# A two-layer hybrid trunk on one core: residual loads spread, gate-stage work moved to VectorE, attention's weights requested one output earlier, the last product in two halves

## The chip, the cores and the metric

One NeuronCore of a Trainium2 chip runs the whole program in one launch. Five engines run side by side, each through its own instruction stream in order: TensorE (PE, with its weight loads shown apart as PEld), VectorE (DVE), ScalarE (ACT), GpSimd (POOL) and SyncE (SP), which here only issues DMA transfers. The metric is the device time of one execution in microseconds, less being better.

## The reference

The activations are `x` (1024 tokens, 1024 features). Layer 0 mixes with an RWKV-7 group and a gated DeltaNet group, layer 1 with chunked softmax attention. Each layer then has a squared-ReLU MLP and a gated addition of a per-layer embedding:

```python
h = rmsnorm(x, norm_mix_g[i])
...                                   # mixer: even layers two recurrent groups, odd layers attention
x = x + mix
hf = rmsnorm(x, norm_ffn_g[i])
x = x + jnp.square(jax.nn.relu(hf @ mlp_w1[i])) @ mlp_w2[i]
x = x + rmsnorm(p[i] @ ple_w_proj[i], ple_norm_g[i]) * jax.nn.sigmoid(x @ ple_w_gate[i])
```

All is float32. The kernel splits each operand into a high part (type fp32r) and a low rest and forms a product from three matmuls.

## The kernel before

The residual lives transposed: eight *rows* of 128 features by 1024 tokens, `x[0]` to `x[7]`, each worked on in two halves of 512 tokens (`hs[0]`, `hs[1]`). `x[0..2]` share the tile `xw0`, `x[3..5]` the tile `xw1`, and `x[6]`, `x[7]` are tiles of their own; the order and the profile print them without the digit, as `xw` and `x`.

A layer is a mixer and then `tail(i, ...)`, which the change is in. The tail does, in this order:

- the mixer's output projection, which leaves the residual in DRAM as `xh` (first halves) and `xm` (second halves);
- the MLP's first product with seven block products in place of eight (`product`), its results stored as `hb` by ScalarE's DMA queue (`store`, L1427) after the row factor `rs` (`normed`, L1422);
- the load of the residual back from DRAM into `x` (L1542 and L1543, SyncE);
- the MLP's second product: a first group done plainly (`plain`, sixteen half outputs of 12 matmuls, each added to `x` by VectorE in `add_to`, L1550, after which `between` starts loads and splits for what follows), and then sixteen blocks in the seven-product form;
- the gate stage: eight outputs `n` of 24 matmuls a half. `ev_gate` takes a half from PSUM: tanh (ScalarE, L1644), the embedding `pn` loaded (L1646) and multiplied by the row factor `prs` (GpSimd, L1647), combined (VectorE, L1648), added to `x` (L1649), stored. In layer 0 it also scales and splits the new row for attention (`xg`, L355 on ScalarE and L356 on VectorE) and adds its squares into `accs` (L1659 on ScalarE, L1660 on GpSimd).

Layer 1's attention starts with the products of `xg` with `wq` (`attn_in`); the first head pair's `wq` is loaded from within layer 0's gate stage (`load_qkv`: load L1878, high part L1879 on ScalarE, low part L1880 on VectorE) into the tiles `xw0` (high) and `xw1` (low), those of rows 0 to 5. After three token groups `row_stats` forms the sums of `accs` on TensorE (`st`) and VectorE turns them into factors (`ms`, L378 and following); only then can the three PSUM banks be emptied.

A list scheduler with its own timeline orders each engine's instructions, so a change in one place can shift orders in another. Every product of the program is recorded at one line (L180), every transpose at L195. Pools give out buffers in turn; an instruction waits until the last user of its buffer is done. DMA transfers report through a small set of semaphores that SyncE's and ScalarE's queues share in turn.

Of the kernel before, what the change touches and what calls it, by code (L numbers as in the profile page):

```python
# [11 lines left out]
AF = mybir.ActivationFunctionType  # L12
ALU = mybir.AluOpType
# [7 lines left out]
NK = D // P  # L21
HB = 512
# [90 lines left out]
class Trunk:  # L113
# [213 lines left out]
    def dense_part(self, w, acts, evac, order=None):  # L327
        hi, lo = w
        order = order or list(range(len(acts)))
        ps = self.bank()  # L330
        for k in order:
            x = acts[k]
            self.mm3(ps, hi[:, k * P:(k + 1) * P], lo[:, k * P:(k + 1) * P], x[:, 0, :], x[:, 1, :],
                     k == order[0], k == order[-1])
            yield 0
        if self.late is not None:
            self.late.append(lambda: evac(ps))
            n = len(self.late)
            if n in self.plan:
                self.plan[n]()  # L340
            if n == max(self.plan):
                late, self.late = self.late, None
                for f in late:
                    f()
        else:
            evac(ps)
# [866 lines left out]
    def tail(self, i, xsrc):  # L1213
# [9 lines left out]
        nc, tc, a = self.nc, self.tc, self.a  # L1223
        V, A, G = nc.vector, nc.scalar, nc.gpsimd
        last = i == 1
        hs = [slice(0, HB), slice(HB, T)]
        with ExitStack() as es:
            self.psd = 2 * self.psd[0:1] + 6 * [es.enter_context(self.pool(f"psdt{i}", 6, space=PSUM))]
            pB = es.enter_context(self.pool(f"actB{i}"))
            pB = [pB.tile([P, 2, T], F32R, tag=f"r{q}", name="r") for q in range(8)]  # L1230
# [5 lines left out]
            def place(dt, far=False, tag="a"):  # L1236
                if far:
                    return late.tile([P, 2, T], dt, tag=tag, name="late")
                return self.act([P, 2, T], dt, tag)
# [4 lines left out]
            def ring(views):  # L1244
                state = [0]

                def f():
                    state[0] += 1
                    return views[(state[0] - 1) % len(views)]
                return f  # L1250
# [5 lines left out]
            def tiles_x(dt):  # L1256
                xw = [self.xp.tile([P, 3, T], dt, tag=f"xw{q}", name=f"xw{q}") for q in range(2)]
                return ([xw[k // 3][:, k % 3, :] for k in range(6)] +
                        [self.xp.tile([P, T], dt, tag=f"x{k}", name=f"x{k}") for k in (6, 7)])
# [11 lines left out]
            accs = [self.accp.tile([P, HB], F32, tag=f"acc{hf}", name="acc") for hf in range(2)]  # L1271
# [13 lines left out]
            def weights(src, raw, hl):  # L1285
                nc.sync.dma_start(out=raw, in_=src)
                split(hl, raw)
                return hl[:, 0], hl[:, 1]
# [80 lines left out]
            for n in range(NK):  # L1369
# [3 lines left out]
                else:  # L1373
                    w = self.w_next if (i, n) == (0, 2) else weights(a[f"w_out{i}"][n], wr[n % 2], wo[n % 2])
# [7 lines left out]
            scr = ring([v for t in lt[0:2] for v in quarters(t)])  # L1382
            rs = self.pre.tile([P, T], F32, tag="ph", name="rs")
            sq = {}
# [3 lines left out]
            def product(p, m, banks):  # L1388
                c, first = prep[p][1][m], chain[m] not in banks
                if first:  # L1390
                    banks[chain[m]] = self.bank()
                ps = banks[chain[m]]
                for j in range(4):
                    o, z = slice(j * P, j * P + P), cmb[m][j]
                    self.mm3(ps, c[:, 0, o], c[:, 1, o], z[:, 0], z[:, 1], first and j == 0, j == 3, not first)
                return ps
# [94 lines left out]
            for p in range(16):  # L1491
# [5 lines left out]
                for q, m in enumerate(order):  # L1497
                    ps = product(p, m, banks)
# [28 lines left out]
                    if (p, q) in sums:  # L1527
                        n = sums.index((p, q))
# [9 lines left out]
                        V.tensor_tensor(rs, rs, rs, op=ALU.mult)  # L1538
                    yield 0
            x = tiles_x(F32)  # L1540
            for k in range(NK):
                nc.sync.dma_start(out=x[k][:, hs[0]], in_=self.xh[k])  # L1542
                nc.sync.dma_start(out=x[k][:, hs[1]], in_=self.xh2[k])  # L1543
            xf = pB
            areas[6], areas[2], areas[7], areas[3], areas[4] = pq[8:12], pq[12:16], cmb[4], pq[0:4], pq[4:8]
            braw = ring([self.accp.tile([P, HB], F32, tag=f"acc{q}", name="braw") for q in range(2)] + quarters(place(F32)))
            areas[1], areas[5] = [[c for q in qs for c in parts(place(F32R, True, f"r{q}"))] for qs in ((2, 3), (0, 1))]
# [24 lines left out]
            todo2 = [lambda: raws2(0)] + [lambda m=m: prepare2(0, m) for m in order]  # L1572

            def start_blocks(n, hf):
                for _ in range(2 if n < 4 else 1):
                    if todo:
                        todo.pop(0)()
                if n >= 4 and todo2:
                    todo2.pop(0)()
            yield from plain(0, h0, start_blocks)  # L1580
            for f in todo + todo2:
                f()
# [5 lines left out]
            xf = [pB[q] for q in (4, 6, 0, 2, 5, 7, 1, 3)]  # L1588
# [4 lines left out]
            for n in range(NB + 4):  # L1593
# [3 lines left out]
                for s, m in enumerate(order):  # L1597
# [3 lines left out]
                    ps, c = banks[chain[m]], prep2[n][1][m]  # L1601
                    for j, slot in enumerate(slots):
                        o, z = slice(j * P, j * P + P), areas[m][slot]
                        self.mm3(ps, c[:, 0, o], c[:, 1, o], z[:, 0], z[:, 1], first and j == 0, slot == slots[-1], not first)
                    e, hf = goes[m]
# [24 lines left out]
            prs = self.pre.tile([P, T], F32, tag="ph", name="prs")  # L1630
            pn2 = self.pre.tile([P, 2, HB], F32, tag="pl", name="pn")
# [6 lines left out]
            scr = ring(quarters(lt[3]))  # L1638

            def ev_gate(n):  # L1640
                def f(hf, ps):
                    sl = hs[hf]
                    sg = scr()
                    A.activation(sg, ps, AF.Tanh, scale=0.5)  # L1644
                    pn = pn2[:, hf]
                    nc.sync.dma_start(out=pn, in_=self.pnd[n][:, hf, :])  # L1646
                    G.tensor_tensor(pn, pn, prs[:, sl], op=ALU.mult)  # L1647
                    V.scalar_tensor_tensor(sg, sg, 1.0, pn, op0=ALU.add, op1=ALU.mult)  # L1648
                    V.tensor_tensor(x[n][:, sl], x[n][:, sl], sg, op=ALU.add)  # L1649
                    if last:  # L1650
                        nc.sync.dma_start(out=a["out"][n, :, sl], in_=x[n][:, sl])
                    else:
                        nc.sync.dma_start(out=self.xd[n][:, sl], in_=x[n][:, sl])
                        if hf == 0:
                            xg.append(place(F32R, tag="b" if n < 2 else "a"))
                        self.split_scaled(xg[n], x[n][:, sl], self.vec("mixg", 8 + n), sl)
                        if n:
                            sq = scr()
                            A.activation(sq, x[n][:, sl], AF.Square)  # L1659
                            G.tensor_tensor(accs[hf], accs[hf], sq, op=ALU.add)  # L1660
                        else:
                            A.activation(accs[hf], x[n][:, sl], AF.Square)
                return f
            wl = ring(halves(lt[1]))

            def load_gate(n):

                far = n > 1 and not last
                raw = wl() if far else raw_b()
                return weights(a["w_gate"][i, n], raw, lt[2 * (n % 2)] if far else place(F32R))  # L1670
            w = {n: load_gate(n) for n in range(2)}
            for n in range(NK):
                if n == NK - 1 and not last:
                    self.wq = self.load_qkv(0, wl)
                yield from self.dense(w.pop(n), xf, ev_gate(n))
                if n + 2 < NK:
                    w[n + 2] = load_gate(n + 2)
            if not last:
# [507 lines left out]
```

## Time and profile before

| | |
|---|---|
| time, median of 3 runs | 3074.66 us (3072.01 to 3075.01) |
| the profiled execution | 3086.63 us |
| its span | 3084.8 us |
| TensorE busy | 2970.1 us, 96% |
| VectorE busy | 2209.9 us, 72% |
| ScalarE busy | 1486.2 us, 48% |
| GpSimd busy | 552.9 us, 18% |
| mean granted TensorE clock | 0.974 |

Times are microseconds from the span's start. In a row of the timeline the first two numbers are start and duration; the brackets give how long the engine had been idle and what released it. A row of the windows lists the busy time of each engine with its instruction count, then the granted TensorE clock, the busy share of the DMA engines and what they moved. In this execution layer 0's tail ends at about 1694, layer 1's attention runs from there to about 2310, and layer 1's tail to the end.

### The profile page before, as it was taken

The numbers are of one execution on the slowest core, as the hardware profiler recorded it, in microseconds if no ns is written. First come the engines' busy times: TensorE is split into PE (matmuls) and PEld (weight loads), VectorE is DVE, ScalarE is ACT, GpSimd is POOL, SyncE is SP. The second block draws the span as 40 slices with busy tenths as digits, with TensorE's granted clock in tenths as the row PEclk, the third lists the DMA queues.
The fourth block names the chain that finished last, engine by engine and source line by source line (L and its number), as shares of the span: only waits on it lengthen the run. The fifth ranks groups of instructions, "written<-read, shape, count | busy, mean of one in ns | idle before, by whom it ended". The sixth has DMA issues, their size and how long they took to land.

```text
span 3084.8 us, 47290 instructions
## 1 busy us (share of the span) xinstructions
PE 2970.1 (96%) x17254; PEld 2457.1 (80%) x17254; DVE 2209.9 (72%) x4546; ACT 1486.2 (48%) x2957; POOL 552.9 (18%) x985
## 2 busy tenths in 40 slices
PE   8999999999999999999999999999999999999999
PEld 6777777777777888788887988898878888888887
DVE  7556766667758777788887676676768777788883
ACT  4333433434437555544444465565757555544441
POOL 5434442443500000000005111111210000000002
PEclk9899999999999999999999999999999999999999
DMA  4212112212346444754424211110256444654433
GB/s 145 64 55 62 54 49 75 61 55 68 110 157 227 162 150 151 262 166 151 151 95 131 70 44 40 43 61 23 75 181 223 163 154 153 237 190 150 150 103 116
DMA packets 194857, 368.49 MB, mean 119 GB/s; under 512 B 46800, under 2 KB 49088, under 8 KB 194624
## 3 DMA queue, kind: packets, MB, share of 16 engines
q1 hardware_dynamic: 163808, 309.35, 31.4%
q10 hardware_dynamic: 30816, 56.11, 4.7%
q8 instruction: 136, 2.23, 0.3%
q14 instruction: 97, 0.79, 0.1%
HBM read 268.86 MB, written 96.53 MB: 118 GB/s over the span
## 4 chain that ended last, share of the span: by engine, by line
PE 71%; DVE 14%; DMA 6%; ACT 4%; issue 2%; POOL 1%; SPq 0%; ACTq 0%; DVEq 0%; POOLq 0%
PE dps L180 57%; PE ch L180 2%; PE po L180 2%; DVE act L1283 2%; PE pm L180 1%; PE iz L180 1%; PE pt L195 1%; DMA late<-in_w 1%; PE sn L180 1%; PE tp L180 1%; DMA late<-hd 1%; DVE late L1431 1%; DMA wraw<-in_w_out 1%; PE py L180 1%; DVE wlo L307 1%
## 5 line engine op out<-in xcount | busy, mean ns | idle before, releaser
L180 PE MATMUL dps<-r,act 128*128 128x512 f32 x3720 | 872.9, 392 | 2.0 <-DVE xw L1550 0.8
L180 PEld LDWEIGHTS dps<-r,act 128*128 128x128 f32 x3720 | 698.0, 188 | 157.0 <-issue 1.2
L180 PE MATMUL dps<-xg,whi 128*128 128x512 f32 x1280 | 436.0, 421 | 11.2 <-ACT whi L306 7.4
L1647 POOL TENSOR_TENSOR pn<-pn,prs 128x512 f32<-128x512 f32 x32 | 47.3, 1483 | 1542.6 <-ACT prs L389 1419.5
L180 PE MATMUL dps<-wq,act 128*128 128x384 f32 x1536 | 307.8, 347 | 13.8 <-DVE vs L1909 6.0
L180 PEld LDWEIGHTS dps<-xg,whi 128*128 128x128 f32 x1280 | 236.2, 197 | 62.2 <-ACT whi L306 7.6
L180 PEld LDWEIGHTS dps<-wq,act 128*128 128x128 f32 x1536 | 269.6, 193 | 17.7 <-DVE vs L1909 7.6
L180 PE MATMUL dps<-xg,wlo 128*128 128x512 f32 x640 | 260.7, 407 | 2.6 <-DVE wlo L307 2.6
L1282 ACT CAST act<-act 128x512 fp32r<-128x512 f32 (+2 forms) x281 | 159.3, 600 | 142.0 <-PE dps L180 59.8
L1283 DVE TENSOR_TENSOR act<-act 128x512 fp32r<-128x512 f32 (+2 forms) x281 | 180.1, 669 | 4.6 <-ACT act L1282 4.6
L180 PE MATMUL dps<-act 128*128 128x512 f32 x720 | 176.5, 393 | 2.0 <-DVE late L1404 2.0
L1282 ACT CAST act<-late 128x512 fp32r<-128x512 f32 x210 | 123.7, 620 | 100.4 <-PE dps L180 73.8
L180 PE MATMUL dps<-late,act 128*128 128x512 f32 x672 | 166.6, 392 | 0.0
L180 PEld LDWEIGHTS dps<-act 128*128 128x128 f32 x720 | 136.2, 189 | 32.1 <-DVE late L1404 2.4
L1283 DVE TENSOR_TENSOR act<-late,act 128x512 fp32r<-128x512 f32 x210 | 139.1, 687 | 31.1 <-ACT act L1282 30.9
L180 PEld LDWEIGHTS dps<-xg,wlo 128*128 128x128 f32 x640 | 125.0, 195 | 32.5 <-DVE wlo L307 3.8
L180 PEld LDWEIGHTS dps<-late,act 128*128 128x128 f32 x672 | 126.0, 188 | 27.7
L180 PE MATMUL dps<-xw,act 128*128 128x512 f32 x576 | 145.9, 392 | 0.2 <-ACT act L1282 0.2
L1550 DVE TENSOR_TENSOR xw<-xw,dps 128x512 f32<-128x512 f32 x192 | 130.0, 682 | 17.3 <-PE dps L180 17.2
L306 ACT CAST whi<-wraw 128x1024 fp32r<-128x1024 f32 (+1 forms) x79 | 81.8, 1035 | 107.6 <-PE dps L180 77.1
L180 PEld LDWEIGHTS dps<-xw,act 128*128 128x128 f32 x576 | 107.9, 188 | 24.4 <-ACT act L1282 0.7
L180 PE MATMUL po<-ptile,vs 128*128 128x256 f32 (+1 forms) x576 | 106.8, 295 | 15.5 <-ACT ptile L352 9.7
(488 smaller groups left out, 5600.7 us busy)
## 6 DMA issues: line engine op xcount, KB each, us to landing
hb<-late ACTq DMA_DIRECT2D x196, 256.0 KB
act<-hb SPq DMA_DIRECT2D x158, 256.0 KB
late<-in_w SPq DMA_DIRECT2D x60, 512.0 KB
act<-in_w SPq DMA_DIRECT2D x112, 256.0 KB
wraw<-in_w_in SPq DMA_DIRECT2D x55, 512.0 KB
braw<-hb SPq DMA_DIRECT2D x80, 256.0 KB
wraw<-in_w_out SPq DMA_DIRECT2D x21, 512.0 KB
wraw<-in_w_qkv SPq DMA_DIRECT2D x21, 512.0 KB
```

Of the source, the lines that this page charges most:

```text
L180: return self.begin(self.nc.tensor.matmul(out, lhsT, rhs, start=start, stop=stop, skip_group_check=again))
L195: return self.begin(self.nc.tensor.transpose(out, in_, ident))
L306: nc.scalar.copy(hi, raw)
L307: nc.vector.tensor_tensor(lo, raw, hi.bitcast(F32), op=ALU.subtract)
L1282: A.copy(hi, s)
L1283: V.tensor_tensor(lo, s, hi.bitcast(F32), op=ALU.subtract)
L1431: V.tensor_tensor(t, u, v, op=ALU.subtract)
L1550: V.tensor_tensor(x[n][:, hs[hf]], x[n][:, hs[hf]], ps, op=ALU.add)
L1647: G.tensor_tensor(pn, pn, prs[:, sl], op=ALU.mult)
```

## The change

Four edits, all in `tail` but one line of `dense_part`. The residual's rows 0 to 2 are loaded where all eight were; the others are each requested after the first half of an output of the plain group, three outputs ahead, and pinned behind what was traced before them on SyncE. In the gate stage the two GpSimd operations go to VectorE. `load_qkv(0, ...)` is called before output 6 instead of before output 7. In layer 1 the second half of the last gate product is computed as two products of 256 tokens, each evacuated on its own (`ev_end`).

```diff
     def dense_part(self, w, acts, evac, order=None):
-        ps = self.bank()
+        ps = self.bank()[:, 0:acts[0].shape[-1]]
...
-            for k in range(NK):
-                nc.sync.dma_start(out=x[k][:, hs[0]], in_=self.xh[k])
-                nc.sync.dma_start(out=x[k][:, hs[1]], in_=self.xh2[k])
-            xf = pB
+
+            def load_res(n):
+                for hf, src in enumerate((self.xh[n], self.xh2[n])):
+                    tc.keep_in_program_order(nc.sync.dma_start(out=x[n][:, hs[hf]], in_=src))
+            for n in range(3):
+                load_res(n)
...
             def start_blocks(n, hf):
+                if hf == 0 and n + 3 < NK:
+                    load_res(n + 3)
...
-                    G.tensor_tensor(pn, pn, prs[:, sl], op=ALU.mult)
+                    V.tensor_tensor(pn, pn, prs[:, sl], op=ALU.mult)
...
-                            G.tensor_tensor(accs[hf], accs[hf], sq, op=ALU.add)
+                            V.tensor_tensor(accs[hf], accs[hf], sq, op=ALU.add)
...
+            def ev_end(c, ps):
+                sg, n = scr()[:, 0:HB // 2], NK - 1
+                A.activation(sg, ps, AF.Tanh, scale=0.5)
+                if c.start == HB:
+                    pn = pn2[:, 1]
+                    nc.sync.dma_start(out=pn, in_=self.pnd[n][:, 1, :])
+                    V.tensor_tensor(pn, pn, prs[:, hs[1]], op=ALU.mult)
+                V.scalar_tensor_tensor(sg, sg, 1.0, pn2[:, 1, c.start - HB:c.stop - HB], op0=ALU.add, op1=ALU.mult)
+                V.tensor_tensor(x[n][:, c], x[n][:, c], sg, op=ALU.add)
+                nc.sync.dma_start(out=a["out"][n, :, c], in_=x[n][:, c])
...
-                if n == NK - 1 and not last:
+                if n == NK - 2 and not last:
                     self.wq = self.load_qkv(0, wl)
-                yield from self.dense(w.pop(n), xf, ev_gate(n))
+                if last and n == NK - 1:
+                    yield from self.dense_part(w[n], [z[:, :, hs[0]] for z in xf], lambda ps: ev_gate(n)(0, ps))
+                    for q in (2, 3):
+                        c = slice(q * HB // 2, (q + 1) * HB // 2)
+                        yield from self.dense_part(w[n], [z[:, :, c] for z in xf], lambda ps: ev_end(c, ps))
+                else:
+                    yield from self.dense(w.pop(n), xf, ev_gate(n))
```

By the changed kernel's line numbers the residual's loads are L1544, `add_to` L1552, the product with `prs` L1651, the two operations behind it L1652 and L1653, the sum of squares L1664, and the low parts of attention's weights L1901. TensorE's order in the middle of attention comes out of the scheduler differently too.

## The prediction

> **What bounds the kernel now.** I read the totals first, then who TensorE waited for in the four places that the diff touches, then short windows around each wait.
>
> ```profile
> span 3084.8 us, 47290 instructions
> PE 2970.1 (96%) x17254; PEld 2457.1 (80%) x17254; DVE 2209.9 (72%) x4546; ACT 1486.2 (48%) x2957; POOL 552.9 (18%) x985
> ```
>
> TensorE is busy for 96% of the span, so only time in which it stands still or runs slowly can be saved, and the tail stages have little of that. TensorE's waits there, one answer each for 1240 to 1340, 1560 to 1720 (two rows) and 2640 to 2760 (columns: total us, times, longest):
>
> ```profile
> PE dps L180 <- DVE late L1404: 2.0, 1, 2.0
> ...
> PE dps L180 <- ACT act L355: 4.5, 1, 4.5
> PE dps L180 <- DVE vs L1909: 2.8, 1, 2.8
> ...
> PE dps L180 <- DVE r L1283: 0.7, 1, 0.7
> ```
>
> The first and last lie where the residual is loaded (layer 0, layer 1); the other two lie where layer 0's gate stage hands over to attention. Windows around them show what follows such a wait (width; busy us of PE, PEld, DVE, ACT, POOL; granted TensorE clock; DMA share; GB/s):
>
> ```profile
> 1283.00:1287.00 4.00, 2.76 (x13) 1.92 (x11) 0.74 (x3) 0.63 (x1) 0.00 (x0) 1.00 1.05 389
> 1287.00:1292.00 5.00, 4.28 (x12) 3.38 (x13) 4.17 (x8) 1.26 (x2) 0.00 (x0) 0.66 0.74 281
> ...
> 1694.00:1698.00 4.00, 3.85 (x12) 3.34 (x13) 2.85 (x4) 1.78 (x4) 2.24 (x3) 0.57 0.73 223
> ...
> 1714.00:1718.00 4.00, 4.00 (x16) 4.00 (x16) 2.73 (x12) 0.00 (x0) 1.04 (x1) 0.58 0.02 4
> 1720.00:2310.00 590.00, 543.99 (x3387) 510.15 (x3386) 422.38 (x1325) 361.93 (x897) 92.82 (x84) 0.97 0.20 64
> ...
> 2676.00:2680.00 4.00, 3.74 (x16) 3.10 (x17) 2.54 (x4) 0.42 (x1) 0.00 (x0) 1.00 1.05 396
> ```
>
> After the waits of 2.0, 4.5 and 2.8 us the clock falls to 0.66, 0.57 and 0.58 in the window behind; after the 0.7 us it does not. TensorE is busy in those windows, so the lost clock is lost time: (1 - 0.66) x 5 = 1.7, (1 - 0.57) x 4 = 1.7, (1 - 0.58) x 4 = 1.7 us. A wait that goes takes its slow stretch along.
>
> The Trainium skill's page "TensorE: Matmul & The Clock Gate" (section "Why this matters for your kernels") warns of idle gaps above about 3 us only. By it the slow stretches behind 2.0 and 2.8 us would not hang on those gaps, and the result would be 3.4 us later than mine. The trace disagrees: clock 0.66 behind a gap of 2.0.
>
> **Residual's loads.** Layer 0's stall, step by step:
>
> ```profile
> 1280.13 0.54 SPq L1543 DMA_DIRECT2D x<-xm  x1
> ...
> 1285.34 0.33 ACTq L1427 DMA_DIRECT2D hb<-late  x1
> 1285.71 0.63 ACT L1410 ACTIVATE late<-late 128x512 f32<-128x512 f32 x1 [3.29 <-DMA x<-xm]
> ```
>
> ScalarE could not issue a store until the last residual half had landed, 5 us after its issue; L1410 stood behind that store, VectorE's L1404 behind L1410, and TensorE behind L1404. At 389 GB/s the transfers were saturated. On SyncE's queue, at the start of the first plain group of layer 0, `xw1`/`x6`/`x7` being residual rows 3 to 7, before stands
>
> ```order
> L1542 DMA xw_12789<-xh 128x512
> L1543 DMA xw_12789<-xm 128x512
> L1542 DMA x_12790<-xh 128x512
> L1543 DMA x_12790<-xm 128x512
> L1542 DMA x_12791<-xh 128x512
> L1543 DMA x_12791<-xm 128x512
> L1482 DMA act<-hb 128x512 x2
> ```
>
> and now, from the same place (rows 0 to 4 go out ahead of it in both):
>
> ```order
> L1482 DMA act<-hb 128x512 x2
> L1482 DMA braw<-hb 128x512
> L1441 DMA w_12896<-in_w 128x512 x2
> L1544 DMA xw_12789<-xh 128x512
> L1544 DMA xw_12789<-xm 128x512
> L1482 DMA act<-hb 128x512 x2
> L1441 DMA w_12986<-in_w 128x512 x2
> L1544 DMA x_12791<-xh 128x512
> L1482 DMA act<-hb 128x512
> L1544 DMA x_12791<-xm 128x512
> L1482 DMA act<-hb 128x512
> ```
>
> Six loads of 256 KB leave the burst: 1.57 MB at 389 GB/s is 4.0 us, more than ScalarE's 3.3 us wait. I take layer 0's stall as gone: 2.0 + 1.7 = **3.7 us** (bounds 0 and 3.7). Layer 1 has the same burst (396 GB/s) and 0.7 us: **0.7 us** (bounds 0 and 0.7). Late next could be row 6: it comes last of all, behind twelve further transfers and the braw pair before which it now stands:
>
> ```profile
> 1306.76 0.32 SPq L1482 DMA_DIRECT2D braw<-hb  x1
> ...
> 1319.87 0.69 DVE L1550 TENSOR_TENSOR x<-x,dps 128x512 f32<-128x512 f32 x1
> ```
>
> Issued at about 1306.8 and used at 1319.9, it has 13 us, against 5 for a landing in the burst. Free.
>
> **Gate stage.** VectorE, ScalarE and GpSimd in 1620 to 1680, grouped by line (count | busy us, mean ns | idle before, releaser):
>
> ```profile
> L1648 DVE SCALAR_TENSOR_TENSOR late<-late,pn 128x512 f32<-128x512 f32 x11 | 14.7, 1334 | 5.6 <-ACT late L1644 5.6
> L1649 DVE TENSOR_TENSOR xw<-xw,late 128x512 f32<-128x512 f32 x10 | 11.9, 1188 | 0.3
> L356 DVE SCALAR_TENSOR_TENSOR act<-xw,vecs,act 128x512 fp32r<-128x512 f32 x11 | 9.5, 860 | 6.7 <-ACT act L355 6.5
> ...
> L1880 DVE TENSOR_TENSOR wq<-late,wq 128x1024 fp32r<-128x1024 f32 x2 | 2.7, 1382 | 2.3 <-DMA xd<-xw 2.3
> ...
> L1660 POOL TENSOR_TENSOR acc<-acc,late 128x512 f32<-128x512 f32 x10 | 17.8, 1780 | 7.9 <-ACT late L1659 7.9
> L1647 POOL TENSOR_TENSOR pn<-pn,prs 128x512 f32<-128x512 f32 x12 | 17.7, 1479 | 43.0 <-DMA pn<-pnd 39.4 <-DMA xd<-xw 3.6
> ```
>
> The end of the kernel shows the pace of a half output (ScalarE's tanh comes every 5.49 us) and the same VectorE work with GpSimd idle, 0.69 us instead of 1.19:
>
> ```profile
> 3074.03 0.60 ACT L1644 ACTIVATE late<-dps 128x512 f32<-128x512 f32 x1 [4.89 <-PE dps L180]
> ...
> 3079.52 0.60 ACT L1644 ACTIVATE late<-dps 128x512 f32<-128x512 f32 x1 [4.89 <-PE dps L180]
> ...
> 3080.95 0.69 DVE L1649 TENSOR_TENSOR x<-x,late 128x512 f32<-128x512 f32 x1
> ```
>
> So the GpSimd work slows VectorE, by 1.33 - 0.69 on L1648 and 1.19 - 0.69 on L1649. Moved over, each half costs VectorE four operations of 0.69 us and L356's 0.86 at most, half a gate weight's split (1.23 / 2, the 128x1024 row below) and 0.6 waiting for L355 (6.5 / 11): 2.8 + 0.9 + 0.6 + 0.6 = 4.9, under 5.49. VectorE keeps up; its lag does not build.
>
> In the order of VectorE at the end of that stage, before, `x_12790` being row 6, `wq` attention's first weights:
>
> ```order
> L356 SCALAR_TENSOR_TENSOR act<-xw_12789,vecs,act 128x512
> L1880 TENSOR_TENSOR wq_15749<-late,wq_15748 128x1024 x2
> L1648 SCALAR_TENSOR_TENSOR late<-late,pn 128x512
> L1649 TENSOR_TENSOR x_12790<-x_12790,late 128x512
> L356 SCALAR_TENSOR_TENSOR act<-x_12790,vecs,act 128x512
> L1880 TENSOR_TENSOR wq_15749<-late,wq_15748 128x1024
> ```
>
> and now:
>
> ```order
> L356 SCALAR_TENSOR_TENSOR act<-xw_12789,vecs,act 128x512
> L1664 TENSOR_TENSOR acc<-acc,late 128x512
> L1651 TENSOR_TENSOR pn<-pn,prs 128x512
> L1901 TENSOR_TENSOR wq_15678<-late,wq_15677 128x1024 x2
> L1652 SCALAR_TENSOR_TENSOR late<-late,pn 128x512
> L1653 TENSOR_TENSOR x_12790<-x_12790,late 128x512
> L356 SCALAR_TENSOR_TENSOR act<-x_12790,vecs,act 128x512
> L1651 TENSOR_TENSOR pn<-pn,prs 128x512
> L1664 TENSOR_TENSOR acc<-acc,late 128x512
> L1901 TENSOR_TENSOR wq_15678<-late,wq_15677 128x1024
> ```
>
> The weights' low parts (L1880, now L1901) have not moved: they are written over rows 3 to 5 and wait for row 5's store (2.3 us, `DMA xd<-xw`). "One output ahead" by itself is therefore worth 0, and row 6 still queues behind that wait.
>
> What TensorE needs at the hand-over:
>
> ```profile
> 1685.61 3.83 PE L180 MATMUL dps<-wq,act 128*128 128x384 f32 x21
> ...
> 1694.35 0.58 ACT L1644 ACTIVATE late<-dps 128x512 f32<-128x512 f32 x1
> ```
>
> The last gate product is done at about 1685.6, its tanh starts at 1694.35: a lag of 8.7 us. TensorE runs 21 matmuls, then waits from 1689.4 for row 7's first half. That half's product ends 5.49 us before 1685.6, at 1680.1; tanh 0.6, L1652 and L1653 1.4, L355 and L356 some 1.5 us make 1683.6, and the third L1901 with one acc and one pn in between (1.2 + 1.4) at most 1686.2. That is 3.2 us early, so the wait goes: 4.5 + 1.7 = **6.2 us** (bounds: 0, and 6.2).
>
> The second wait, on TensorE, ScalarE and VectorE:
>
> ```profile
> 1704.78 1.84 PE L180 MATMUL st<-ones,acc 128*128 128x1 f32 x16
> ...
> 1706.48 4.41 PE L180 MATMUL dps<-wq,act 128*128 128x384 f32 x24
> ...
> 1706.81 1.05 ACT L1879 CAST wq<-wraw 128x1024 fp32r<-128x1024 f32 x1 [3.62 <-DMA wraw<-in_w_qkv]
> 1707.89 1.23 DVE L1880 TENSOR_TENSOR wq<-wraw,wq 128x1024 fp32r<-128x1024 f32 x1 [3.41 <-ACT wq L1879]
> 1709.04 0.16 DVE L378 TENSOR_SCALAR ms<-st 128x8 f32<-128x8 f32 x1
> ...
> 1713.73 14.35 PE L180 MATMUL dps<-wq,act 128*128 128x384 f32 x72 [2.84 <-DVE vs L1909]
> ```
>
> The row statistics are ready at 1706.6, but L378 stands behind the split of head pair 1's third weight and starts 2.4 us late; SyncE issued that weight's load behind the stores of row 7. Those stores come 8.7 us earlier when the lag goes, TensorE 6.2, so this chain gains 2.5 us on TensorE, just what L378 was late: from L378 to TensorE's restart are 4.7 us, TensorE has 4.3 of work meanwhile, and 0.4 are left, too short for a slow stretch (0.7 had none). Gain 2.8 + 1.7 - 0.4 = **4.1 us** (bounds 0 and 4.5).
>
> **Last product.** The only 256-wide rows are in attention and the final blocks (TensorE; VectorE and ScalarE by line):
>
> ```profile
> 2129.32 1.06 PE L180 MATMUL po<-ptile,vs 128*128 128x256 f32 x7
> ...
> L1476 DVE TENSOR_TENSOR act<-act 128x256 f32<-128x256 f32 x9 | 3.6, 418 | 0.0
> ...
> L1904 ACT ACTIVATE qk<-dps,rscol 128x256 f32<-128x256 f32 x64 | 30.3, 474 | 63.1 <-PE dps L180 59.3 <-DVE rscol L294 3.5
> ```
>
> Behind the last matmul the chain shortens by (0.60 - 0.47) + 2 x (0.69 - 0.42) = 0.7 us. 48 matmuls at 1.06 / 7 = 0.15 us at most are 7.3 us against 5.5; at half the width's share, 5.5. I take 0.3 more, near the latter, since the 1.06 includes one matmul's full latency. Net **0.4 us** (bounds -1.1 and 0.7).
>
> A rule speaks against this: the same page (section "The mechanism") says that a weight load runs beside matmuls in flight only when the row groups differ. Then 24 more loads would each add their own time, some 4.5 us by the 0.19 us that a load takes here, and I would forecast 3067. The trace disagrees: seven 256-wide matmuls with their seven loads take 1.06 us.
>
> **What the scheduler shuffles.** TensorE's order in attention changes from the fifth step on. Before:
>
> ```order
> L180 MATMUL sf<-F_17658,F_18107 128x256
> L195 MATMUL pt<-ident,pb 128x128 x2
> L180 MATMUL po<-ptile,vs 128x256 x7
> L180 MATMUL sf<-F_17658,Ql 128x256
> L195 MATMUL pt<-ident,pb 128x128 x4
> ```
>
> and now:
>
> ```order
> L180 MATMUL sf<-F_17658,F_18107 128x256
> L180 MATMUL sf<-F_17658,Ql 128x256
> L195 MATMUL pt<-ident,pb 128x128 x2
> L180 MATMUL po<-ptile,vs 128x256 x7
> L195 MATMUL pt<-ident,pb 128x128 x4
> ```
>
> Such swaps recur over three head pairs and fall into the two patterns of these stretches of before, one head pair each:
>
> ```profile
> 1881.50:1953.60 72.10, 65.22 (x407) 62.51 (x406) 50.30 (x162) 41.98 (x107) 11.19 (x10) 0.93 0.14 43
> ...
> 2021.50:2087.20 65.70, 61.44 (x410) 58.59 (x408) 50.46 (x165) 41.65 (x107) 11.28 (x10) 1.00 0.16 47
> 2087.20:2154.80 67.60, 62.63 (x408) 59.97 (x406) 45.13 (x156) 38.75 (x104) 10.15 (x10) 0.97 0.07 23
> ```
>
> The new order repeats the beginning of the first (72.1) more often, with an end nearer the third (67.6); I estimate one pair 3 us longer: **-3 us**, bounds -9 (two pairs at 72.1 for 67.6) and +4.5 (the first at 67.6).
>
> **Sum.** 3.7 + 0.7 + 6.2 + 4.1 + 0.4 - 3 = 12.1 us off the profiled execution's 3086.6 (3084.8 span and 1.8 around it). That execution lies 12 us above the median of 3074.66; none of the terms scales with that, so 3074.66 - 12.1 = **3062.5 us**.
>
> **The rivals.** *Attention eats half:* order costs 9 instead of 3, or the 4.1 stays with its wait: gain 6 to 8, 3066.5 to 3068.5. For it: 46 us of idle and clock 0.97 in the attention window leave room. Chance 0.2, half of it within the threshold once a second small loss joins. *Attention gains:* order worth 1 to 4 us the other way, gain 16 to 19, 3056 to 3059: 0.14. *Slower, VectorE sets layer 0's gate pace:* if the long operations come from something other than GpSimd, each half costs 1.33 + 1.19 + 0.86 + 0.6 + 0.6 and two new ones at 1.2, 7.0 us against 5.49: 16 x 1.5 = 24 us of lag. 4.2 of before's 8.7 are free (8.7 - 4.5), so it costs 24 - 8.7 = 15 more and takes the 10.3 of the hand-over; with 3.7 + 0.7 + 0.4 - 3 left, +13, 3088. It beats before from 0.7 us of excess in a half. Against it: 0.69 with GpSimd idle. 0.08 with smaller mishaps of that sign. *It does nothing:* stalls come back elsewhere at equal size, 3072 to 3076: 0.04.
>
> **How the numbers follow.** 0.2% is 6.1 us, about what a measurement of this kernel can tell from no change: faster means below 3068.5. The forecast holds 0.54 with its own range 3058 to 3066.5. Faster: 0.54 + 0.14 + 0.1 = 0.78; same 0.14; slower 0.08. The range 3055.5 to 3069.5 leaves out the slow and the idle case and the edges.
>
> **What would show it.** No TensorE wait on L1404 behind the residual's loads and clock 1.00 there; no wait on L355 after the first 21 matmuls of `wq`; L1652 and L1653 at about 0.7 us; L378 right behind `st`; the last tanh on 128x256. Wrong if attention grows by more than 9 us or TensorE waits in the gate stage.

## The result, and the profile after

The changed kernel takes 3081.42 us (median of 13 runs, 3071.31 to 3087.13) against 3075.01 us for the kernel before in the same comparison: a ratio of 1.0023 with a 95% interval of [1.0013, 1.0033]. It is slower by about 7 us (4 to 10 by the interval) where 12 us of gain were forecast. The profiled execution took 3085.99 us. That is 4.6 us above its kernel's median, and before's profiled execution lies 12 us above the median that the prediction took, so the two spans are almost the same; the profiles are compared stage by stage. The totals of after:

```profile
span 3084.3 us, 47305 instructions
PE 2967.2 (96%) x17278; PEld 2453.5 (80%) x17278; DVE 2213.2 (72%) x4594; ACT 1485.2 (48%) x2958; POOL 481.9 (16%) x939
```

The work left GpSimd as planned (552.9 to 481.9 us) and VectorE grew by only 3.3. The gate stage of layer 0 (1620 to 1680, grouped by line; count, busy us, mean ns, idle before and its releaser) has the durations that the prediction named, 0.69 us each. What is new is the last column of L1651: VectorE itself now waits for the load of `pn`.

```profile
L1651 DVE TENSOR_TENSOR pn<-pn,prs 128x512 f32<-128x512 f32 x13 | 9.0, 691 | 9.9 <-DMA pn<-pnd 9.7
L1652 DVE SCALAR_TENSOR_TENSOR late<-late,pn 128x512 f32<-128x512 f32 x11 | 7.5, 684 | 0.0
```

TensorE's waits in the tails, from the same windows as in the prediction (1240 to 1340, then 1560 to 1720; total us, times, longest). In 2640 to 2760 nothing is left.

```profile
PE dps L180 <- ACT late L1400: 0.8, 1, 0.8
```

```profile
PE dps L180 <- DVE vs L1930: 2.6, 1, 2.6
PE dps L180 <- ACT act L355: 1.2, 1, 1.2
PE dps L180 <- ACT late L1282: 0.6, 1, 0.6
PE dps L180 <- ACT late L1648: 0.4, 1, 0.4
```

The waits of the tails did shrink: 2.0 to 0.8 at the residual, 4.5 to 1.2 + 0.4 at the first hand-over place, 2.8 to 2.6 at the second. One of 0.6 on L1282, at 1591, is new. The loss lies in attention. The windows of three head pairs, from the start of the same transpose on TensorE, first the pair of before that the prediction does not show, then the three of after (width; busy us of PE, PEld, DVE, ACT, POOL; granted clock; DMA share; GB/s):

```profile
1953.60:2021.50 67.90, 63.27 (x407) 61.35 (x406) 47.05 (x157) 42.04 (x107) 9.38 (x10) 0.95 0.14 45
```

```profile
1871.30:1942.40 71.10, 63.95 (x408) 60.97 (x406) 50.52 (x165) 41.60 (x107) 11.56 (x10) 0.95 0.14 43
1942.40:2014.90 72.50, 65.57 (x409) 62.71 (x407) 49.66 (x163) 41.83 (x107) 10.57 (x10) 0.92 0.13 43
2014.90:2085.90 71.00, 63.95 (x409) 61.33 (x407) 48.39 (x159) 41.56 (x107) 11.29 (x10) 0.96 0.14 44
```

Before, the three took 72.1 + 67.9 + 65.7 = 205.7 us; after, 71.1 + 72.5 + 71.0 = 214.6, 8.9 more. The new order repeats the slow pattern three times. TensorE's two largest waits in 1740 to 2310, of before and then of after, show the idle part of it:

```profile
PE po L180 <- ACT ptile L352: 9.7, 11, 1.8
PE pt L195 <- ACT pb L2034: 4.2, 4, 1.5
```

```profile
PE po L180 <- ACT ptile L352: 13.9, 14, 1.8
PE pt L195 <- ACT pb L2055: 6.7, 5, 1.8
```

The products `po` and the transposes `pt` come too early for ScalarE's softmax steps three more times and once more: 6.7 us of idle time together over the whole stretch. Smaller waits shrank, so TensorE's idle time in 1740 to 2310 grew from 44.5 to 49.0 us. Inside the three pairs, width less TensorE's busy time grew from 15.8 to 21.1 us, and the time lost to the clock (width times what is missing to 1.00, summed) from 8.4 to 12.2: together 9.1, which is the 8.9 within the rows' rounding.

### The profile page after: what moved, and what is told of

Its sections match the earlier page's. It is cut to its first block, busy times and chain, and to the rows that moved or that the text cites. A ratio compares the mean times of both kernels' runs of the same rounds, so it can differ in the third digit from the quotient of the medians.

```text
span 3084.3 us, 47305 instructions
## 1 busy us (share of the span) xinstructions
PE 2967.2 (96%) x17278; PEld 2453.5 (80%) x17278; DVE 2213.2 (72%) x4594; ACT 1485.2 (48%) x2958; POOL 481.9 (16%) x939
## 4 chain that ended last, share of the span: by engine, by line
PE 76%; DVE 11%; DMA 6%; ACT 3%; issue 2%; POOL 1%; SPq 0%; ACTq 0%; DVEq 0%; POOLq 0%
PE dps L180 62%; PE ch L180 2%; PE po L180 2%; PE pm L180 2%; PE iz L180 1%; PE pt L195 1%; PE sn L180 1%; DMA pn<-pnd 1%; PE tp L180 1%; DMA wraw<-in_w_out 1%; DVE act L1283 1%; PE py L180 1%; DVE wlo L307 1%; PE pp L180 1%; DMA act<-in_w 1%
## 5 line engine op out<-in xcount | busy, mean ns | idle before, releaser
L180 PE MATMUL dps<-r,act 128*128 128x512 f32 (+1 forms) x3744 | 873.2, 390 | 2.0 <-DVE act L1283 1.1
L1282 ACT CAST act<-act 128x512 fp32r<-128x512 f32 (+2 forms) x281 | 159.5, 600 | 146.3 <-PE dps L180 66.1
L1282 ACT CAST act<-late 128x512 fp32r<-128x512 f32 x210 | 123.7, 620 | 98.8 <-PE dps L180 71.9
L180 PEld LDWEIGHTS dps<-xg,wlo 128*128 128x128 f32 x640 | 123.8, 193 | 32.1 <-DVE wlo L307 3.7
L1552 DVE TENSOR_TENSOR xw<-xw,dps 128x512 f32<-128x512 f32 x192 | 129.7, 680 | 18.9 <-PE dps L180 18.7
```

Source lines behind the costliest of these rows:

```text
L180: return self.begin(self.nc.tensor.matmul(out, lhsT, rhs, start=start, stop=stop, skip_group_check=again))
L1282: A.copy(hi, s)
L1552: V.tensor_tensor(x[n][:, hs[hf]], x[n][:, hs[hf]], ps, op=ALU.add)
```

## The experiments

All ran beside the kernel before on the same chip, but not all on one chip; the ratio and its 95% interval compare each with before on its own chip. In each, TensorE's order in attention was read from the trace, over its 3533 matmuls; the fifth column says whose it was. The last three columns are of the one profiled execution: TensorE's idle time and granted clock in 1740 to 2310 (the kernels reach attention up to 16 us apart, so the stretch does not hold quite the same work), and the length of the hand-over, from the first product with `wq` to the end of the 72 matmuls behind the second wait.

| run | median us | before us | ratio, interval | order in attention | idle us | clock | hand-over us |
|---|---|---|---|---|---|---|---|
| before | | | | before's | 44.5 | 0.96 | 42.5 |
| after | 3081.42 | 3075.01 | 1.0023 [1.0013, 1.0033] | after's | 49.0 | 0.96 | 37.7 |
| e1 | 3072.18 | 3075.79 | 0.9986 [0.9968, 1.0003] | before's | 43.5 | 0.98 | 38.2 |
| e2 | 3085.80 | 3075.79 | 1.0033 [1.0017, 1.0049] | after's | 49.7 | 0.97 | 42.3 |
| e3 | 3071.30 | 3075.79 | 0.9977 [0.9961, 0.9993] | before's | 44.0 | 0.98 | 41.0 |
| e4 | 3077.07 | 3076.60 | 1.0006 [0.9993, 1.0019] | after's | 47.7 | 0.95 | 37.9 |
| e5 | 3076.71 | 3076.60 | 1.0005 [0.9992, 1.0019] | after's | 47.6 | 0.95 | 32.5 |
| e6 | 3065.40 | 3076.60 | 0.9972 [0.9960, 0.9984] | a third | 42.8 | 0.96 | 32.8 |
| e7 | 3071.31 | 3076.60 | 0.9992 [0.9978, 1.0006] | before's | 44.3 | 0.99 | 45.7 |
| e8 | 3071.81 | 3077.30 | 0.9980 [0.9970, 0.9990] | before's | 44.5 | 0.97 | 38.7 |
| e9 | 3081.09 | 3077.30 | 1.0014 [0.9998, 1.0030] | after's | 47.8 | 0.95 | 38.3 |
| e10 | 3084.87 | 3077.30 | 1.0024 [1.0012, 1.0036] | after's | 49.5 | 0.96 | 39.8 |
| e11 | 3075.46 | 3077.30 | 0.9998 [0.9981, 1.0015] | before's | 44.7 | 0.98 | 42.4 |
| e12 | 3063.71 | 3075.76 | 0.9962 [0.9945, 0.9979] | before's | 43.2 | 0.97 | 32.1 |

By the medians, no kernel with the new order is below before and none with before's order is above it, though six of the intervals (e1, e4, e5, e7, e9, e11) include 1. The idle time in attention keeps the two orders apart: 47.6 to 49.7 us with the new one, 43.2 to 44.7 with before's. The clock there does so less: 0.95 to 0.97 against 0.96 to 0.99, in one execution each.

### Whose fault is the order? e1, e2, e3 and e10

The very first output's product with `prs` in layer 0, one instruction for each half, turns out to switch the order. e1 is the changed kernel with that output's product left on GpSimd.

```diff
-                    V.tensor_tensor(pn, pn, prs[:, sl], op=ALU.mult)
+                    (V if last or n >= 1 else G).tensor_tensor(pn, pn, prs[:, sl], op=ALU.mult)
```

> The changed kernel, except that layer 0's first gate output (n = 0, both halves) is multiplied by prs on GpSimd as before. Those two instructions are enough for the scheduler to give attention on TensorE the order of before. Theory 'order' (the tails gain what TensorE's place in the trace shows, 7 to 11 us by early attention, and the reshuffled attention gives it back): about 3065 us, 10 below before. Rival 'tails' (the moved tail work itself costs, the order is neutral): like the changed kernel, about 3081 us.

e2 is the kernel before with only that product moved to VectorE.

```diff
-                    G.tensor_tensor(pn, pn, prs[:, sl], op=ALU.mult)
+                    (G if last or n else V).tensor_tensor(pn, pn, prs[:, sl], op=ALU.mult)
```

> The kernel before, except that layer 0's first gate output (both halves) is multiplied by prs on VectorE. Attention on TensorE then gets the changed kernel's order; everything else of the change is absent. Theory 'order': before plus 6.4 plus about 10, so 3088 to 3093 us. Rival 'tails': like before, 3075 us within 2.

e3 is the changed kernel with both operations back on GpSimd (`V.` to `G.` at L1651 and L1664), so three of the four edits.

> Residual's loads, attention's weights and the last product as in the change, but the gate stage's two operations on GpSimd as before; attention keeps the order of before. Theory 'order': the residual's part (3.7 + 0.7) and the end (0.4) are gained, the hand-over is not: about 3070 us. Rival 'tails': those parts are worth nothing or cost, 3075 us or more.

e10 is the changed kernel once more, unedited.

> The changed kernel once more, unedited, beside the others on one chip. Theory 'order': as measured, 5 to 8 us above before's median on this chip, and 9 above e8's; TensorE's idle time in attention again 49 us. Rival 'a draw' (the 3081 came from unlucky placements of the slow clock): within 2 us of before, since e4, the same program but for one split, stood 0.5 above before.

e2 loses 10.0 us against before (5 to 15 by the ratio's interval) with every other edit missing; 12 to 17 were expected. On the other side, the changed kernel stands 9.2 above e1 (measured at different times) and, on one chip, e10 stands 13.1 above e8, which has e1's order and one moved instruction. The theory "order" holds in direction, and e10, slower by as much once more (1.0024), speaks against a chance draw. The whole stretch 1740 to 2310, of e2 and then of e1:

```profile
1740.00:2310.00 570.00, 520.30 (x3264) 486.79 (x3263) 409.73 (x1290) 349.63 (x874) 91.23 (x82) 0.97 0.20 64
```

```profile
1740.00:2310.00 570.00, 526.53 (x3287) 488.67 (x3287) 409.01 (x1270) 352.96 (x870) 89.50 (x81) 0.98 0.22 73
```

The three head pairs of e2:

```profile
1877.30:1946.90 69.60, 62.88 (x408) 59.72 (x406) 50.50 (x165) 41.65 (x107) 11.54 (x10) 0.97 0.14 45
1946.90:2017.30 70.40, 63.23 (x407) 60.68 (x406) 49.60 (x162) 41.77 (x107) 10.68 (x10) 0.96 0.13 44
2017.30:2088.00 70.70, 63.63 (x408) 60.92 (x406) 49.27 (x162) 41.64 (x107) 11.29 (x10) 0.96 0.15 44
```

TensorE idles 49.7 us in e2's stretch, 43.5 in e1's and 44.5 in before's, so 5 to 6 us of the loss are idle time. In the three pairs it idles 21.0 us in e2, as in after (21.1), and 15.8 in before. The time that the clock costs does not repeat like that: by these rows it is 7.7 us in e2's pairs, below before's 8.4 and after's 12.2. How much of the rest of the 10 us hangs on the order is not shown. And e1 fell short of its expectation too: 3072 where 3065 was expected. The tails gave 3.6 (e1) and 4.5 (e3) by the medians, not 15. Where the rest went is the second question.

### Why the hand-over still waits: the rows of after, and e4, e7

VectorE, ScalarE, SyncE and TensorE around row 7 in the profile of after, in order of time (start, duration, in brackets the idle time before and its releaser):

```profile
1681.36 0.68 DVE L1652 SCALAR_TENSOR_TENSOR late<-late,pn 128x512 f32<-128x512 f32 x1
...
1682.07 0.32 SPq L1650 DMA_DIRECT2D pn<-pnd  x1
...
1683.76 3.83 PE L180 MATMUL dps<-wq,act 128*128 128x384 f32 x21
...
1683.96 0.58 ACT L1648 ACTIVATE late<-dps 128x512 f32<-128x512 f32 x1
...
1685.38 0.69 DVE L1651 TENSOR_TENSOR pn<-pn,prs 128x512 f32<-128x512 f32 x1 [1.07 <-DMA pn<-pnd]
...
1686.60 0.68 DVE L1652 SCALAR_TENSOR_TENSOR late<-late,pn 128x512 f32<-128x512 f32 x1
...
1688.04 0.72 ACT L355 ACTIVATE act<-x,vecs 128x512 fp32r<-128x512 f32 x1 [3.51 <-DVE x L1653]
...
1688.82 0.62 PE L180 MATMUL dps<-wq,act 128*128 128x384 f32 x2 [1.23 <-ACT act L355]
```

Read it as a circle. L1652 of one half ends at 1682.04 and frees a half of `pn`; its load goes out at 1682.07; L1651 can start 3.3 us later; and only behind that L1651, which belongs to the *following* half, stands L1652 of the half that is due. From 1681.36 to 1686.60 the circle takes 5.24 us, hardly less than the 5.49 of a half on TensorE, so a lag is not worked off: the last tanh (1689.19) starts 5.4 us behind the end of its product, at 1683.76, where the products with `wq` begin. Before, GpSimd waited for the load, and VectorE's work on the other half did not stand behind it.

The second wait, further on in the same profile:

```profile
1699.98 1.84 PE L180 MATMUL st<-ones,acc 128*128 128x1 f32 x16
1701.68 4.41 PE L180 MATMUL dps<-wq,act 128*128 128x384 f32 x24
...
1701.74 1.05 ACT L1900 CAST wq<-wraw 128x1024 fp32r<-128x1024 f32 x1 [2.88 <-DMA wraw<-in_w_qkv]
...
1702.83 1.23 DVE L1901 TENSOR_TENSOR wq<-wraw,wq 128x1024 fp32r<-128x1024 f32 x1 [2.70 <-ACT wq L1900]
1703.97 0.16 DVE L378 TENSOR_SCALAR ms<-st 128x8 f32<-128x8 f32 x1
...
1708.65 12.78 PE L180 MATMUL dps<-wq,act 128*128 128x384 f32 x72 [2.56 <-DVE vs L1930]
```

The statistics are there when the 24 matmuls begin, at 1701.7, and L378 starts only 2.3 us later, behind the third split of head pair 1. e4 (the changed kernel) and e7 (e3) give that split to GpSimd:

```diff
-            nc.vector.tensor_tensor(wl[:, j, :], raw, wh[:, j, :].bitcast(F32), op=ALU.subtract)
+            (nc.gpsimd if pr == 1 and j == 2 else nc.vector).tensor_tensor(wl[:, j, :], raw, wh[:, j, :].bitcast(F32), op=ALU.subtract)
```

> All four edits; only the third low part of head pair 1's weights goes to GpSimd, which leaves the row statistics (L378) no split to stand behind. TensorE's order in attention is then the one of before. Theory 'blockers' (the second hand-over wait stayed because L378 still stands behind the third split, which waits for its load): the wait of 2.6 to 2.8 us falls to 0.2 to 0.5, TensorE restarts 2.3 us earlier than in e1 counted from the last gate product, and the time is 3068 to 3071 (e1's 3072.2 less 2 to 4). Rival 'another in its place' (the banks' emptying or something else is just as late): the wait stays above 1.5 us and the time at e1's 3072.

> As e3 (the gate stage's two operations stay on GpSimd, the other three edits made, before's order in attention), with the third low part on GpSimd as in e4. Theory 'blockers': the first hand-over wait (4.5 us, on L355) stays, the second (2.0 us here) falls to 0.3: 3067.5 to 3070 against e3's 3071.3. Rival 'GpSimd is too late with it' (its split waits for the work before it there, and head pair 1's first product waits): 3071 to 3075.

e4's expectation took before's order for granted; its trace has after's, so only its hand-over can be read against it. There the wait stayed: 2.61 us in e4, 2.63 in e7, whose 3071.3 us miss the 3067.5 to 3070 expected. L378 did start at once (1703.32 in e4). But then, VectorE and GpSimd in e4:

```profile
1704.93 2.32 DVE L292 TENSOR_TENSOR rsw<-rscol 128x8 f32<-128x8 f32 x1
...
1704.85 2.39 POOL L1901 TENSOR_TENSOR wq<-wraw,wq 128x1024 fp32r<-128x1024 f32 x1 [6.01 <-ACT wq L1900]
```

A 128x8 operation that takes 0.17 us elsewhere in that chain took 2.32, until GpSimd's split was over. In e7 it was another 128x8 operation of the chain (L289, 2.35 us beside a split of 2.41). The blocker was removed and its time came back as a collision of the two engines. (That e4's ratio is nevertheless lower than the changed kernel's 1.0023 and 1.0024 its trace does not explain; the intervals overlap.) The Trainium skill's page "SBUF — State Buffer" (section "Who interferes with whom") says that a VectorE operation with two inputs in SBUF and a GpSimd operation that reads SBUF take a shared port as a lock, for the whole instruction. The row of e4 agrees: 2.32 us, until GpSimd's instruction ended. In e7 the operation held had one input, so it does not take two here.

### Freeing one wait, then both: e8, e9, e5, e6 and e12

e8 is e1 with one product put back behind the L1652 that it stood ahead of:

```diff
-                    (V if last or n >= 1 else G).tensor_tensor(pn, pn, prs[:, sl], op=ALU.mult)
+                    op = (V if last or n >= 1 else G).tensor_tensor(pn, pn, prs[:, sl], op=ALU.mult)
+                    if not last and n == 7 and hf == 1:
+                        tc.keep_in_program_order(op)
```

> e1 (before's order in attention, all four edits but the very first product with prs) with one instruction of VectorE moved: row 7's second product with prs (L1651) now stands behind L1652 of row 7's first half, ahead of which it waited for its own load. Theory 'a load in VectorE's stream': the waits of TensorE on L355 and L1648 at the hand-over (1.5 and 0.4 us in e1) go, the second wait (on the row statistics, 2.8) stays between 1 and 3; the time is 2 us under e1's 3072.2, 3068.5 to 3071. Rival 'the tanh chain sets it': the 1.5 us stay and so does 3072.

TensorE's waits of e1 (1660 to 1702), and then of e8 (1660 to 1715):

```profile
PE dps L180 <- DVE vs L1930: 2.8, 1, 2.8
PE dps L180 <- ACT act L355: 1.5, 1, 1.5
PE dps L180 <- ACT late L1648: 0.4, 1, 0.4
```

```profile
PE dps L180 <- DVE vs L1932: 4.4, 1, 4.4
PE dps L180 <- ACT late L1648: 0.4, 1, 0.4
```

The wait on L355 is gone, as the theory says, and the second grew from 2.8 to 4.4: 4.7 us in all in e1, 4.8 in e8, and the hand-over takes 38.2 us in e1 and 38.7 in e8. So the trace shows none of the 2 us that were expected; the times (0.9986 and 0.9980 of before, on two chips) are too close to tell. The two waits are one chain. Counted from the first product with `wq`, TensorE reaches `st` after 13.4 us in place of 16.5, 3.1 sooner; the high part of the third weight, behind whose split L378 stands, comes after 17.0 in place of 18.5, only 1.5 sooner.

e9 is the changed kernel with output 7's two products pinned (`n == 7`), e5 is e9 with the third split on GpSimd too, e6 is e5 with the pin for every output of layer 0 (`n >= 0`).

> All four edits of the change, with output 7's two products with prs pinned behind what was traced before them on VectorE and nothing on GpSimd; TensorE's order in attention is e6's third order. Theory 'order and load' (e6's gain is the third order's low idle time in attention plus the freed hand-over): the idle time in attention is again near 42.8 us, the first hand-over wait is 0, the second 1 to 2.5 as the third split is back on VectorE: 3065 to 3068. Rival 'e6 gained by its other parts' (third split on GpSimd, products of outputs 0 to 6 pinned): 3069 to 3073.

> All four edits with the changed kernel's own order in attention; two blockers are taken out of VectorE's stream at the hand-over: for output 7 the product with prs is pinned behind what was traced before it (so it no longer waits for its load ahead of the previous half's L1652), and the third low part goes to GpSimd as in e4. Theory 'blockers': the waits on L355 and L1648 (1.2 and 0.4 us) and the one on the statistics (2.6 us) all go to 0.4 together, attention still costs its 10 us more: 3075.5 to 3078. Rival 'order alone decides' (the hand-over's waits are made up later): 3080 to 3082. Rival 'the reshuffle was not the cause': 3066 to 3069, since the tails' full gain would then show.

> All four edits, the product with prs pinned for every output of layer 0's gate stage, third low part on GpSimd. TensorE's order in attention is a third one, neither before's nor the changed kernel's. Theory 'blockers': VectorE no longer waits for pn's load in the gate stage, the tanh follows its product at once, no hand-over wait over 0.5 us. Theory 'order': the time then hangs on what this third order costs; with before's cost 3064 to 3068, with the changed kernel's 3074 to 3078, and the idle time of TensorE in attention (43.5 or 49) says which. Rival 'tanh lag is set by ScalarE's own order': the lag of 5 us and the 1.2 us wait stay.

e9's expectation assumed e6's order, but its trace has after's; its second wait is 4.84 us, its hand-over 38.3 and its time 3081, which repeats e8's lesson under the other order. e5 frees both: one wait of 1.08 us is left (0.4 was expected), the hand-over falls to 32.5, and attention keeps the new order's idle time (47.6); its 3076.7 lies in the range expected. e6 frees both and draws a third order: its wait at the hand-over is 1.40 us (at most 0.5 was expected), TensorE idles 570 - 527.2 = 42.8 us in 1740 to 2310, and it took 3065.4, 0.9972 of before (e3's interval overlaps).

e12 is e8 with the third split on GpSimd: before's order, no blocker.

> e8 (before's order in attention, row 7's second product with prs behind L1652 of the first half) with the third low part of head pair 1's weights on GpSimd as well, so that neither of the two blockers of the hand-over is left. Theory 'one chain' (freeing the first wait alone only passed its time on to the second: 1.5 + 0.4 + 2.8 in e1, 0.4 + 4.4 in e8): the second wait falls to 1 to 1.5 as in e5 and e6, hand-over's waits together under 2, and the time 3 us or a little more under e8's 3071.8: 3066 to 3069. Rival 'the port' (the GpSimd split comes while VectorE works out the row factors and holds one of its small operations for 2.3 us, as in e4): the second wait stays at 2.5 or more, 3071.

```profile
1679.67 12.70 PE L180 MATMUL dps<-wq,act 128*128 128x384 f32 x72
1692.21 1.84 PE L180 MATMUL st<-ones,acc 128*128 128x1 f32 x16
1693.91 4.41 PE L180 MATMUL dps<-wq,act 128*128 128x384 f32 x24
1698.99 12.78 PE L180 MATMUL dps<-wq,act 128*128 128x384 f32 x72 [0.67 <-DVE vs L1932]
```

These are TensorE's rows of e12, from the first product with `wq` on: 72 matmuls without a stop, and 0.7 us of waiting where before had 7.4. The same work, to the end of the second 72, took 32.1 us in place of 42.5: 10.4 us, which is what the prediction's two hand-over terms came to. GpSimd's split now starts at 1696.76, after the last of the row factors (1696.10), so the collision does not happen either. 40 us around the hand-over, of before and then of e12:

```profile
1680.00:1720.00 40.00, 32.48 (x165) 30.36 (x164) 23.73 (x43) 13.35 (x24) 18.51 (x18) 0.91 0.41 134
```

```profile
1680.00:1720.00 40.00, 37.78 (x224) 36.85 (x223) 20.81 (x49) 14.68 (x30) 12.81 (x15) 1.00 0.31 99
```

The clock is 1.00 where it was 0.91. (The counts are not of the same work: the products with `wq` begin 5.6 us into the window before, and just ahead of it in e12.) e12 takes 3063.71 us, 0.9962 [0.9945, 0.9979] of before: the lowest ratio of the versions (the intervals of e3, e6 and e8 overlap), better than expected (3066 to 3069), and about 12 us under before (6 to 17). That is the forecast's number, but not its sum: it takes four instructions placed otherwise than in the change (the first output's two products, row 7's second product and one split), and order costs nothing, where the forecast's terms without the 3 us for order make 15.

### The residual alone: e11

The kernel before with the loads spread as in the change and nothing else.

> Before with the residual's loads spread and nothing else; TensorE's order in attention is unchanged. Theory 'idle only' (a wait is worth its idle time; whether a slow clock stretch follows is a draw): 2.0 + 0.7 less the 0.8 that comes late next in layer 0, 2 us under before's median. Theory 'idle and clock' (as forecast): 4.4 us under. Rival 'the loads are late elsewhere': no gain.

Ratio 0.9998 [0.9981, 1.0015]: from 6 us of gain to 5 of loss, so it separates none of the three. What can be read are traces. In e11's the wait of 2.0 us is down to 0.7, and of layer 1's 0.7 there are 0.5 left. And e2 has before's loads. Its stall behind them (1.39 us, 1284.59) is followed by this window:

```profile
1287.00:1292.00 5.00, 5.00 (x23) 4.12 (x22) 3.99 (x7) 2.30 (x4) 0.00 (x0) 1.00 0.60 231
```

Clock 1.00, where the same stall in before (2.0 us) was followed by 0.66. Over 1283 to 1292 the clock is 0.81 in before's profile and 1.00 in all the others.

## Why the prediction was wrong, point by point

**What the scheduler shuffles (-3).** This is the first step that failed, and the size was at fault, not the mechanism. I saw that the new order repeats the first pattern, and estimated one pair 3 us longer. It repeats it in three pairs: +8.9 us in the profile of after, and e2, with nothing else changed, is 10.0 us slower (5 to 15). The bound of -9 that stood beside the estimate was nearly right. What repeats of the 8.9 is the idle part, 5.4 us (5.2 in e2). The step "with an end nearer the third" was an impression from a few rows of order; nothing in the trace of before priced it.

**Hand-over, first wait (6.2).** The durations were right (0.68 and 0.69) and so was "its lag does not build", but it was not worked off either. I counted the products with `prs` as 0.69 us of VectorE and left out that each waits for a load, and that the scheduler sets it one half ahead. The quoted order shows it: L1651 ahead of the weights and of L1652. Row 7's first half was to be ready at most 0.6 us after the first product with `wq` (1686.2 against 1685.6); TensorE got it 5.1 us after (1688.82 against 1683.76). 2.9 of 4.5 us of idle time went, and a slow stretch stayed: the clock is 0.57 in 1690 to 1694. e8 shows that the 1.5 us which e1 still waits there are worth nothing while the second wait stands.

**Second wait (4.1).** Nothing was gained: 2.8 to 2.6, and 3.8 in e10. I let the third load come 8.7 us earlier with the stores; its high part L1900 came 5.1 earlier (1706.81 to 1701.74), and TensorE's `st` 4.8 earlier, so L378 stood behind the split just as long. Together the two terms, forecast at 10.3, were one chain with two blockers. The hand-over's length says it in all the runs: 42.5 us before, 37.7 to 39.8 where the first wait is cut or gone and the second stands, 32.1 to 32.8 where both are freed (e12, e5, e6). So the size was right and the claim that this change frees both was wrong: 4.8 us came in after.

**Residual (3.7 + 0.7).** The stalls went from 2.0 to 0.8 and from 0.7 to nothing, so about 2 us of idle time (after 2310 other small waits came in: 2.2 us of idle time in all where before had 1.6). The slow stretch that I added (1.7) did not follow e2's stall of 1.39 us at the same place; whether the shorter stall is the reason is not shown. And the half that held up ScalarE's store was not the last one, issued at 1280.13: by the semaphore events of before's trace the store waited for row 6's second half, issued at 1279.13, whose last packet reported at 1285.26, and it went out before the last half (1286.62). The term does not hang on which of the two it was. e3, which has the residual, the halves and the earlier weights, is 0.9977 [0.9961, 0.9993], 2 to 12 us; the forecast for these was 4.8.

**Last product (0.4).** Right in sign, but too small. In after, the last products' matmuls, then the tanh of its two quarters:

```profile
3039.72 40.40 PE L180 MATMUL dps<-r,act 128*128 128x512 f32 x200
...
3077.43 0.38 ACT L1671 ACTIVATE late<-dps 128x256 f32<-128x256 f32 x1 [2.12 <-PE dps L180]
3080.15 0.38 ACT L1671 ACTIVATE late<-dps 128x256 f32<-128x256 f32 x1 [2.34 <-PE dps L180]
```

The quarters follow one another in 2.72 us, twice that being 5.44 against 5.49 for a half: 24 more matmuls and weight loads cost nothing, where the sum had 0.3 us, and the 4.5 us that the prediction worked out from a rule on weight loads did not come. (The section "The mechanism" of the Trainium skill's page "TensorE: Matmul & The Clock Gate", from which the rule is quoted, also lets a load for the background weight buffer be pulled ahead, which the prediction left out; no run here shows which case this is.) From TensorE's end to the span's there are 3084.3 - 3080.1 = 4.2 us in place of 5.3 (3084.8 - 3079.5): 1.1 us, beyond the upper bound of 0.7.

**The rivals.** VectorE as the bound of the gate stage was rightly held unlikely. "Order costs 9 instead of 3" and "the 4.1 stays with its wait" were both named, as alternatives; both happened, and the first wait's term came only in part. I had no case in which terms fall together.

**The base.** Taking the terms off the median was sound, but before's 29 runs on one chip spread from 3064.86 to 3089.11, and the profiled execution was a high one. A slow stretch that stands in one profile need not be a term that an edit removes. By the profiles, about 2 us at the residual, 4.8 at the hand-over and 1.1 at the end stand against 8.9 to 10 lost in attention. That leaves a loss of 1 to 2 us where 4 to 10 were measured; the rest is not located.

## What to carry to other kernels

When a list scheduler reorders a dense stage as a side effect, price the whole new order, pattern by pattern, before the edit's own terms, and try to hold the old order while testing: here the engine of one product, two instructions, cost 10 us (5 to 15). When an operation moves to a busier engine, move its wait into the count, and look at what the scheduler has set behind it. Two waits in a row on the same chain are one term: ask of each blocker what TensorE would still wait for if it alone were gone.

## What the runs showed of the hardware

One 128x8 VectorE operation was held for 2.32 us beside a GpSimd subtraction of 2.39 us (0.17 elsewhere): a small operation in a critical chain pays for the whole of GpSimd's instruction. And the slow clock stretches do not follow each stall: 0.66 behind one of 2.0 us, 1.00 behind the same place's 1.39. At the hand-over's second place the length of the wait nearly decides: the 72 matmuls behind it took 12.8 us after waits of 0.67 to 2.79 us (e12, e5, e6, e3, after, e4, e1) and 14.3 to 14.8 after 2.84 to 4.84 (before, e2, e11, e10, e8, e9); e7, with 15.6 after 2.63, is the exception. At the first place it does not: 49 matmuls took 10.3 us after 1.2 to 1.5 + 0.4 us (after, e1, e4) and 8.8 after 2.1 + 0.4 (e10). The limit of about 3 us that the prediction weighed and set aside nearly fits the second place, and not the first. The Trainium skill's page "TensorE: Matmul & The Clock Gate" (section "What's actually happening") has the activity window free-running, so that a stall's place in it would matter; that would fit the spread, but no run here moved a stall within the window, and it stays open. It also stays open why the scheduler's order in attention hangs on the engine of one product in the tail; only that it does was shown.
